# Modulation vectors of a hybrid DiT layer: weights as the stationary operand in plain float32

## The chip, the cores and the metric

The kernel runs on one core of a Trainium2 chip. The metric is the device time of one execution in microseconds (us), median of the runs shown. Engines are named as in the profile: PE (matmuls), PEld (PE's weight loads, which overlap its matmuls), DVE (vector), ACT (scalar), POOL (GpSimd) and SP, which issues most of the DMAs.

## The reference

Two layers of a diffusion backbone act on 1024 latent tokens and 256 context tokens of width 1024. Each layer has one projection into three kinds of heads (latent attention, differential attention, a gated chunk MLP), an output projection, and a convolutional MLP. The change concerns the modulation: shift, scale and gate vectors (six of width 1024 for each layer) made from a condition vector for the latents and another one for the context.

```
s_c = jax.nn.silu(c)
s_cc = jax.nn.silu(c_ctx)
for l in range(DEPTH):
    mod = (s_c @ p["ada_w"] + p["ada_b"])[:, None, :]
    modc = (s_cc @ p["ada_w"] + p["ada_b"])[None, None, :]
    x, xc = layer(x, xc, mod, modc, rows, cols, p, l, l < DEPTH - 1)

def layer(x, xc, mod, modc, ...):
    sh1, sc1, g1, sh2, sc2, g2 = jnp.split(mod, 6, axis=-1)
    y, yc = mixer(x * (1.0 + sc1) + sh1, xc * (1.0 + csc1) + csh1, ...)
    x = layer_norm(DN_ALPHA * x + g1 * y, ...)
    x = layer_norm(DN_ALPHA * x + g2 * conv_ffn(x * (1.0 + sc2) + sh2, p), ...)
```

`ada_w` is 1024 x 6144 for each layer, 50 MB in float32 for both, and it is multiplied by two vectors only.

## The kernel before, in words

**Numbers.** Nearly all matrix products are written as three matmuls of type float32r. Each operand is split into a high part (a rounding copy, mostly on ACT, line 460 `copy`) and a low part (the full value minus the high one, on DVE or POOL, line 457 `low`). Line 447 (`mm`) issues every matmul of this kind. Transposes and a few small products run in plain float32: `ident`, `sel64` (64 moving columns), `sumj`, and the mixing product of the chunk MLP (`wsT`, 64 moving columns).

**Order.** The program is a list of tasks. Each names the engines it may run on with an estimated time, the buffers that it reads and writes, and a key. A scheduler (`Sched.run`) plays the list through with these estimates when the program is built. It gives each task to an engine and thereby fixes the order of instructions on each engine. A changed estimate or a removed task moves other tasks too, among them those that can run on either DVE or POOL.

**Modulation.** The 48 pieces (two layers, six vectors, four quarters) are made by `mod_piece`. A piece is 1024 x 256 of `ada_w`. Its weights are loaded, split into high and low, and are the moving operand: 16 matmuls of 256 columns, in which the stationary operand is `s4`, the silu of both condition vectors as high and low (four columns, shown as `region,s` in the profile). The result, four rows by 256, is copied from PSUM by ACT (`m4`), and two matmuls with the 4 x 2 matrix `sel4` (4 rows, moving 2 columns, plain float32) bring it to columns and add high and low. DVE adds the bias (line 715).

The pieces stand at two kinds of places. Eight of layer 0 (scale and shift of the first norm) are made at the start, in `first_hT`, in blocks of 128 x 1024 (`raws` given), between the first tokens and the first projection weights, whose products need them. The other 40 are filled into the two attention stages (24 into layer 0's, 16 into layer 1's) in blocks of 128 x 512, of which each is loaded, split and multiplied by a task of its own. There PE also has score matmuls, transposes of the probabilities (line 1252) and the products with the values; DVE takes the running minimum of the scores out of PSUM (line 1183) and makes low parts; ACT does the exponentials (line 1188) and high parts.

The instructions of an engine run in the order of the program, so whatever stands behind a waiting matmul on PE waits too.

Of the kernel before, what the change touches and what calls it, by code (L numbers as in the profile page):

```python
# [10 lines left out]
F32 = mybir.dt.float32  # L11
F32R = mybir.dt.float32r
# [8 lines left out]
P = 128  # L21
# [312 lines left out]
def dve_t(n, per=1.042e-3, extra=0.0):  # L334
    return {"dve": per * n + 0.07 + extra}
# [32 lines left out]
def mm_t(count, n):  # L368
    return {"pe": count * max(0.11, 0.4167e-3 * n + 0.0027)}
# [21 lines left out]
class Kern:  # L391
# [248 lines left out]
    def setup(self):  # L640
        nc, c, i = self.nc, self.cst, self.i

        def load(name, shape, key=0):
            t = c.tile(shape, F32, tag=name, name=name)
            self.dma(lambda: t, lambda: i[name], 4 * P * int(np.prod(shape[1:])), w=[name], key=key)
            return t

        cc = load("cT", [P, KD, 2])
        s = c.tile([P, KD, 2], F32, tag="silu", name="silu")
        self.s4 = c.tile([P, KD, 4], F32R, tag="s4", name="s4")  # L650
        self.task(act_t(16), lambda e: nc.scalar.activation(s, cc, AF.Silu), ["cT"], ["silu"])
        self.task(dve_t(16), lambda e: nc.vector.tensor_copy(self.s4[:, :, 0:2], s), ["silu"], ["s4a"])
        self.task(dve_t(16), lambda e: self.low(nc.vector, self.s4[:, :, 2:4], s, self.s4[:, :, 0:2]), ["silu", "s4a"], ["s4"])
        self.sel4 = load("sel4", [4, 2])
        self.modv, self.lnv, self.adab, self.inw = [], [], [], {}
        for l in range(DEPTH):
            self.modv.append(c.tile([P, 6, KD, 2], F32, tag=f"modv{l}", name="modv"))
            t = c.tile([P, 6, KD], F32, tag=f"adab{l}", name="adab")
            self.dma(lambda t=t: t, lambda l=l: i["ada_b"][l], 4 * P * 48, w=[("adab", l)], key=300 * l)
            self.adab.append(t)  # L660
            t = c.tile([P, 4, KD], F32, tag=f"lnv{l}", name="lnv")
            self.dma(lambda t=t: t, lambda l=l: i["lnv"][l], 4 * P * 32, w=[("lnv", l)], key=300)
            self.lnv.append(t)
        self.cv = c.tile([P, 2 * NF, 4], F32, tag="conv", name="conv")
        for name, shape in (("ident", [P, P]), ("sumj", [P, P]), ("sel64", [P, 64])):
            setattr(self, name, load(name, shape, 200))
        self.identr = c.tile([P, P], F32R, tag="identr", name="identr")
        self.task(dve_t(P), lambda e: nc.vector.tensor_copy(self.identr, self.ident), ["ident"], ["identr"], key=200)
        d = self.dr
        self.zd = d.tile([NTOK, 768], F32, tag="zd", name="zd")  # L670
        self.yt = d.tile([NTOK, 512], F32, tag="yt", name="yt")
        self.oT = d.tile([512, NTOK], F32, tag="oT", name="oT")
        self.n1 = d.tile([NTOK, D], F32, tag="n1", name="n1")
        self.n2 = d.tile([SEQ, D], F32, tag="n2", name="n2")
        self.da = [d.tile([7, P, NP, HALF], F32, tag=f"da{l}", name="da") for l in range(DEPTH)]
        self.dc = d.tile([7, P, NP, P], F32, tag="dc", name="dc")
        self.db = [d.tile([4, NP, P, HALF], F32, tag=f"db{l}", name="db") for l in range(DEPTH)]
# [3 lines left out]
        return self.i["ada_w"][l, QUADS[n // 4], n % 4, h]  # L681

    def mod_piece(self, l, n, key=0, raws=None):
        nc = self.nc
        self.s.what = f"mod{l}"
        j, q = QUADS[n // 4], n % 4
        if raws:
            w = [self.weight(None, 1024, self.L, k=4, raw=raws[h]) for h in range(2)]
        else:
            src = [self.mod_src(l, n, h)[:, a:a + 512] for h in range(2) for a in (0, 512)]  # L690
            w = [self.weight(x, 512, self.M, k=2, key=key, acq=True) for x in src]
        kk = KD // len(w)
        ps, m4, pm = self.bank(), self.H(), self.bank(F32, (P, 2, 2))
        for h in range(len(w)):
            def go(e, h=h):
                for k in range(kk):
                    hi, lo = w[h][0][k]()
                    a = self.s4[:, kk * h + k]
                    self.mm(ps[:4, :256], a, hi, h + k == 0, False)
                    self.mm(ps[:4, :256], a, lo, False, kk * h + k == KD - 1)  # L700

            self.task(mm_t(2 * kk, 256), go, ["s4"] + w[h][1], [ps], key=key, acq=[m4] if h == 0 else ())
        self.task(act_t(256), lambda e: self.copy(m4[:4], ps[:4, :256]), [ps], [m4], key=key)

        def sel(e):
            for k in range(2):
                self.mm(pm[:, k], m4[:4, k * P:(k + 1) * P], self.sel4)

        self.task({"pe": 0.25}, sel, [m4, "sel4"], [pm], key=key)
        ks = slice(2 * q, 2 * q + 2)  # L710
        o = self.modv[l][:, j, ks]
        tok = ("modv", l, j, q)

        def fin(e):
            nc.vector.tensor_tensor(out=o, in0=pm.t, in1=self.adab[l][:, j, ks].unsqueeze(2).to_broadcast([P, 2, 2]), op=ALU.add)
            if j in (1, 4):
                nc.vector.tensor_scalar(o, o, 1.0, None, op0=ALU.add)

        self.task({"dve": 0.15}, fin, [pm, ("adab", l)], [tok], key=key)
# [1236 lines left out]
def _arrays(x, c, ctx, c_ctx, ada_w, ada_b, w_in, mla_gq, mla_wuq, mla_gkv, mla_wukv,  # L1956
            diff_lq1, diff_lk1, diff_lq2, diff_lk2, diff_subln_g, sgu_ln_g, sgu_ln_b, sgu_ws, sgu_bs,
            w_o, ln1_g, ln1_b, ffn_wup, ffn_convw, ffn_convb, ffn_wdown, ln2_g, ln2_b):
    L = DEPTH
    a = {}  # L1960
    a["x"], a["ctx"] = x[0], ctx[0]
    a["cT"] = _cols(np.stack([c[0], c_ctx])).transpose(0, 2, 1)
    a["xT"] = np.concatenate([ctx[0], x[0]]).reshape(NTOK, KD, P).transpose(2, 1, 0)
    a["ada_w"] = ada_w.reshape(L, 2, 4, P, 6, 4, 256).transpose(0, 4, 5, 1, 3, 2, 6).reshape(L, 6, 4, 2, P, 1024)
    a["ada_b"] = _cols(ada_b.reshape(L, 6, D)).transpose(1, 0, 2, 3)
    for name in ZCH:
        b, n = ZOFF[name], ZN[name]
        a["w_in_" + name] = w_in[:, :, b:b + n].reshape(L, KD, P, n).transpose(0, 2, 1, 3).reshape(L, P, KD * n)
    wq = mla_wuq.reshape(L, 3, P, NH, 192)
    r = wq[..., 128:]  # L1970
    sw = r.reshape(L, 3, P, NH, 2, 2, 16)[..., ::-1, :].reshape(r.shape)
    a["wq"] = np.concatenate([wq[..., :128], r, sw], -1).transpose(0, 3, 2, 1, 4).reshape(L, NH, P, 768)
    wkv = mla_wukv.reshape(L, 2, P, NH, 256)
    a["wk"] = wkv[..., :128].transpose(0, 3, 2, 1, 4).reshape(L, NH, P, 256)
    a["wv"] = wkv[..., 128:].reshape(L, 2, P, 2, 2, 128).transpose(0, 3, 2, 1, 4, 5).reshape(L, 2, P, 512)
    a["gq"] = _cols(mla_gq).transpose(1, 0, 2)
    a["gkv"] = _cols(mla_gkv).transpose(1, 0, 2)
    a["dl"] = np.stack([diff_lq1, diff_lq2, diff_lk1, diff_lk2], 1)
    a["subln"] = diff_subln_g
    a["sgu_gb"] = np.concatenate([sgu_ln_g, sgu_ln_b], 1)  # L1980
    a["wsT"] = sgu_ws.transpose(0, 3, 1, 2)
    a["bs"] = sgu_bs.transpose(0, 2, 1)
    wo = np.zeros((L, 35, P, 256), np.float32)
    wo[:, :32] = w_o.reshape(L, KD, P, 4, 256).transpose(0, 1, 3, 2, 4).reshape(L, 32, P, 256)
    a["w_o"] = wo.reshape(L, 7, 5, P, 256).transpose(0, 1, 3, 2, 4).reshape(L, 7, P, 1280)
    ln = np.stack([ln1_g, ln1_b, ln2_g, ln2_b], 1)
    a["lnr"] = ln
    a["lnv"] = _cols(ln).transpose(1, 0, 2, 3)
    a["wup"] = ffn_wup.reshape(L, 2, 4, P, 2, NF, P).transpose(0, 4, 1, 5, 3, 2, 6).reshape(L, 2, 2, NF, P, 512)
    cw = np.concatenate([ffn_convw, ffn_convb[:, None]], 1)  # L1990
    a["conv"] = cw.reshape(L, 4, 2, NF, P).transpose(0, 4, 3, 2, 1).reshape(L, P, 2 * NF, 4)
    a["w_down"] = ffn_wdown.reshape(L, NP, 2, P, 2, HALF).transpose(0, 2, 4, 1, 3, 5)
    a["dtab"], a["ktab"], a["cst"] = _rope_tables()
    eye = np.eye(P, dtype=np.float32)
    a["ident"] = eye
    a["sumj"] = np.tile(np.eye(64, dtype=np.float32), (2, 2))
    a["sel64"] = np.tile(np.eye(64, dtype=np.float32), (2, 1))
    a["sel4"] = np.tile(np.eye(2, dtype=np.float32), (2, 1))
    return {k: np.ascontiguousarray(v) for k, v in a.items()}


# [12 lines left out]
```

## Time and profile before

| | |
|---|---|
| median of 3 runs | 3407.99 us (3407.11 to 3412.31) |
| the profiled execution: its time | 3411.25 us |
| its span, first to last instruction | 3409.5 us |
| PE busy | 3186.5 us, 93% of the span |
| DVE, ACT, POOL busy | 79%, 49%, 30% |
| granted TensorE clock, mean | 0.967 of full speed |

The profiled execution is 3.3 us above the median, and 1.75 us of it lie outside its span. The granted clock has two levels here, 1.00 (2.4 GHz) and 0.50 (1.2 GHz); values between are means over a stretch.

### The profile page before, as it was taken

To read this page: it belongs to the slowest core of one execution; us is meant where nothing else is said; L and a number is where in the kernel's file an instruction comes from. 1 tells how busy PE (TensorE), PEld (TensorE's weight loads), DVE (VectorE), ACT (ScalarE), POOL (GpSimd) and SP (SyncE) were. 2 spreads that over 40 slices of the span, in tenths; PEclk is the share of its full clock that TensorE was granted. 3 is DMA by queue.
4 is the path that set the end of the run, shared out by engine and by line. 5 is a ranking of instruction groups with operands and counts; after the bars stand their busy time and mean duration, and the time that the engine had idled before them with its cause. 6 is when DMAs were issued, how large, how long until landed. Compare 5 with 4: busy or idle time off the path is not lost. (4 is left out here: it accounts for less than half of the span.)

```text
span 3409.5 us, 53373 instructions
## 1 busy us (share of the span) xinstructions
PE 3186.5 (93%) x18953; PEld 2785.7 (82%) x18953; DVE 2700.5 (79%) x6407; ACT 1677.3 (49%) x2944; POOL 1028.0 (30%) x631
## 2 busy tenths in 40 slices
PE   7999898998988999999999999989999889999997
PEld 5998887887987888887877898878889867877775
DVE  7567887999768787886687757988998788888687
ACT  5125665666244444544444325665662455545542
POOL 3002554543112111121133302554532232322143
PEclk9999998999999999999999999999999999999998
DMA  6214443442312223225663314353423122323672
GB/s 242 72 52 112 118 124 99 126 108 86 121 69 70 89 72 101 87 86 180 210 204 130 116 58 123 92 135 87 119 88 127 62 80 96 107 98 105 229 258 99
DMA packets 258548, 395.40 MB, mean 116 GB/s; under 512 B 63976, under 2 KB 115688, under 8 KB 258280
## 3 DMA queue, kind: packets, MB, share of 16 engines
q1 hardware_dynamic: 240872, 345.84, 31.4%
q0 software_dynamic: 17408, 46.14, 5.9%
q8 instruction: 149, 2.44, 0.3%
q14 instruction: 119, 0.97, 0.1%
HBM read 311.61 MB, written 126.42 MB: 128 GB/s over the span
## 5 line engine op out<-in xcount | busy, mean ns | idle before, releaser
L447 PE MATMUL t<-region 128*128 128x512 f32 (+4 forms) x15631 | 2853.0, 341 | 137.8 <-DVE region L457 55.0
L447 PEld LDWEIGHTS t<-region 128*128 128x128 f32 x15631 | 2442.1, 192 | 480.0 <-DVE region L457 69.2
L457 DVE TENSOR_TENSOR region<-region 128x512 fp32r<-128x512 f32 (+6 forms) x873 | 760.0, 893 | 176.2 <-ACT region L460 122.7
L460 ACT ACTIVATE region<-region 128x512 fp32r<-128x512 f32 (+4 forms) x944 | 593.9, 663 | 382.8 <-PE t L447 132.5
L460 ACT ACTIVATE region<-t 128x512 fp32r<-128x512 f32 (+4 forms) x948 | 462.1, 514 | 600.0 <-PE t L447 386.3
L457 POOL TENSOR_TENSOR region<-region 128x512 fp32r<-128x512 f32 (+7 forms) x283 | 392.3, 1398 | 1109.3 <-ACT region L460 714.8
L1480 POOL TENSOR_TENSOR region<-region 128x512 f32<-128x512 f32 (+3 forms) x132 | 248.6, 1889 | 823.6 <-DVE region L1667 518.5
L1188 ACT ACTIVATE region<-region,q 128x1280 f32<-128x1280 f32 (+1 forms) x216 | 273.5, 1267 | 175.7 <-DVE q L1187 169.7
L1183 DVE TENSOR_SCALAR_CACHE_REDUCE region<-t 128x512 f32<-128x512 f32 (+1 forms) x600 | 333.7, 584 | 21.3 <-PE t L447 19.1
L457 DVE TENSOR_TENSOR region<-t,region 128x512 fp32r<-128x512 f32 (+1 forms) x529 | 296.9, 595 | 52.8 <-ACT region L460 50.9
L1667 DVE SCALAR_TENSOR_TENSOR region<-region,conv 128x1023 f32<-128x1023 f32 x176 | 231.6, 1325 | 36.7 <-ACT region L1665 36.5
L1480 DVE TENSOR_TENSOR region<-region 128x512 f32<-128x512 f32 (+3 forms) x301 | 226.3, 770 | 2.5 <-DMA da<-region 1.4
L1252 PE MATMUL t<-ident,region 128*128 128x128 f32 x1312 | 184.8, 285 | 24.2 <-DVE region L1225 8.1
L1228 POOL TENSOR_TENSOR region<-region 128x1280 f32<-128x1280 f32 (+1 forms) x68 | 186.8, 2746 | 5.7
L1665 ACT ACTIVATE region<-region,conv 128x1024 f32<-128x1024 f32 x88 | 109.2, 1241 | 159.5 <-DVE region L1648 148.3
L1252 PEld LDWEIGHTS t<-ident,region 128*128 128x128 f32 x1312 | 154.9, 147 | 31.8 <-DVE region L1183 11.0
L1227 POOL TENSOR_SCALAR region<-region,q 128x1280 f32<-128x1280 f32 (+1 forms) x68 | 84.5, 1242 | 210.6 <-DVE q L1222 137.7
L447 PE MATMUL t<-region,s 128*4 128x256 f32 x768 | 119.1, 291 | 17.0 <-DVE region L457 9.2
L447 PEld LDWEIGHTS t<-region,s 128*4 128x4 f32 x768 | 64.6, 87 | 47.4 <-DVE region L457 12.5
L548 POOL TENSOR_TENSOR region<-region 128x1024 f32<-128x1024 f32 x26 | 73.7, 2847 | 95.9 <-DMA region<-n 67.7
L1008 DVE TENSOR_TENSOR region<-t,region 128x256 f32<-128x256 f32 x32 | 13.6, 424 | 107.4 <-PE t L447 107.4
L548 DVE TENSOR_TENSOR region<-region 128x1024 f32<-128x1024 f32 x34 | 62.3, 1841 | 18.2 <-DMA region<-n 17.7
(134 smaller groups left out, 1803.5 us busy)
## 6 DMA issues: line engine op xcount, KB each, us to landing
region<-in_wup SPq DMA_DIRECT2D x176, 256.0 KB, 3.0
region<-in_ada_w SPq DMA_DIRECT2D x160, 256.0 KB, 3.1
da<-region SPq DMA_DIRECT2D x154, 256.0 KB, 3.0
region<-da SPq DMA_DIRECT2D x154, 256.0 KB, 4.1
db<-in_w_down POOLq DMA_DIRECT2D x24, 1408.0 KB, 7.5
region<-db SPq DMA_DIRECT2D x88, 256.0 KB, 4.1
region<-in_w_down SPq DMA_DIRECT2D x66, 256.0 KB, 3.9
n<-region SPq DMA_DIRECT2D x26, 512.0 KB, 3.0
```

Source lines behind the costliest of these rows:

```text
L447: self.nc.tensor.matmul(ps, a, b, start=start, stop=stop, skip_group_check=again)
L457: eng.tensor_tensor(out=out, in0=full, in1=hi.bitcast(F32), op=ALU.subtract)
L460: self.nc.scalar.activation(out, in_, AF.Copy, **kw)
L548: self.task(engs or pool_t(D), lambda e, row=row, op=op: self.vec[e].tensor_tensor(out=x[:, :D], in0=x[:, :D], in1=row.t, op=op), [x, row] ...
L1183: self.task(dve_t(b - a), lambda e: nc.vector.tensor_scalar(p[:, a:b], ps[:, :b - a], -scale, None, op0=ALU.mult, op1=ALU.min, accum_out=n ...
L1188: self.task(act_t(nk, 0.19), lambda e: nc.scalar.activation(p[:, :nk], p[:, :nk], AF.Exp, bias=m.t, scale=-1.0, accum_out=s.t), [p, m], [p ...
L1227: nc.gpsimd.tensor_scalar(p2[:, :nk], p2[:, :nk], cc.t, 0.0, op0=ALU.mult, op1=ALU.add)
L1228: nc.gpsimd.tensor_tensor(out=p1[:, :nk], in0=p1[:, :nk], in1=p2[:, :nk], op=ALU.add)
L1252: nc.tensor.transpose(ps[:, u, j * P:(j + 1) * P], B[key][j][:, (kt + u) * P:(kt + u + 1) * P], self.ident)
L1480: self.task(engs or either(n), lambda e: self.vec[e].tensor_tensor(out=o(), in0=a(), in1=b(), op=op), r, w, **kw)
L1665: self.task(act_t(n, 0.15), lambda e: nc.scalar.activation(t.t, u(0, n), AF.Identity, scale=c[:, 1:2], bias=c[:, 3:4]), r + ["conv"], [t])
L1667: self.task(dve_t(n - 1, extra=0.06), lambda e, d=d: nc.vector.scalar_tensor_tensor(t[:, 1 - d:n - d], u(d, n - 1 + d), c[:, 2 * d:2 * d + ...
```

## The change

The split of the modulation weights, the four-row product, its copy and the selecting product are taken out. Each 128 x 128 block of `ada_w` is now itself the stationary operand, in plain float32, and the moving operand is the silu of both condition vectors: two columns. A piece is 16 matmuls (two groups of 128 outputs, eight blocks along the contraction each) that add up in PSUM, in one task that waits for all of the piece's blocks. DVE's bias add stays. `s4`, its high and low part, and `sel4` go. The estimate of PE's time for a piece, on which the scheduler works, becomes 1.8 us (it was 16 times 0.11 and 0.25).

```
-        self.s4 = c.tile([P, KD, 4], F32R, tag="s4", name="s4")
+        self.silu = s
-        self.task(dve_t(16), lambda e: nc.vector.tensor_copy(self.s4[:, :, 0:2], s), ["silu"], ["s4a"])
-        self.task(dve_t(16), lambda e: self.low(nc.vector, self.s4[:, :, 2:4], s, self.s4[:, :, 0:2]), ["silu", "s4a"], ["s4"])
-        self.sel4 = load("sel4", [4, 2])
...
-        if raws:
-            w = [self.weight(None, 1024, self.L, k=4, raw=raws[h]) for h in range(2)]
-        else:
-            src = [self.mod_src(l, n, h)[:, a:a + 512] for h in range(2) for a in (0, 512)]
-            w = [self.weight(x, 512, self.M, k=2, key=key, acq=True) for x in src]
-        kk = KD // len(w)
-        ps, m4, pm = self.bank(), self.H(), self.bank(F32, (P, 2, 2))
-        for h in range(len(w)):
-            def go(e, h=h):
-                for k in range(kk):
-                    hi, lo = w[h][0][k]()
-                    a = self.s4[:, kk * h + k]
-                    self.mm(ps[:4, :256], a, hi, h + k == 0, False)
-                    self.mm(ps[:4, :256], a, lo, False, kk * h + k == KD - 1)
-
-            self.task(mm_t(2 * kk, 256), go, ["s4"] + w[h][1], [ps], key=key, acq=[m4] if h == 0 else ())
-        self.task(act_t(256), lambda e: self.copy(m4[:4], ps[:4, :256]), [ps], [m4], key=key)
-
-        def sel(e):
-            for k in range(2):
-                self.mm(pm[:, k], m4[:4, k * P:(k + 1) * P], self.sel4)
-
-        self.task({"pe": 0.25}, sel, [m4, "sel4"], [pm], key=key)
+        if not raws:
+            raws = [self.load(self.mod_src(l, n, h)[:, a:a + 512], 512, self.M, key) for h in range(2) for a in (0, 512)]
+        kk = KD // len(raws)
+        pm = self.bank(F32, (P, 2, 2))
+
+        def go(e):
+            for c in range(2):
+                for k in range(KD):
+                    o = k % kk * 256 + c * P
+                    self.mm(pm[:, c], raws[k // kk][:, o:o + P], self.silu[:, k], k == 0, k == KD - 1)
+
+        self.task({"pe": 1.8}, go, ["silu", *raws], [pm], key=key)
```

The order on PE at the start of the program, before (`s_70` is the four-column operand, `sel_71` the selecting matrix; the rows of 512 columns are the first projection):

```order
L447 MATMUL t<-region,s_70 4x256 x24
L447 MATMUL t<-sel_71,region 128x2 x2
L447 MATMUL t<-region,s_70 4x256 x16
L447 MATMUL t<-sel_71,region 128x2 x2
L447 MATMUL t<-region,s_70 4x256 x16
L447 MATMUL t<-sel_71,region 128x2 x2
L447 MATMUL t<-region,s_70 4x256 x8
L447 MATMUL t<-sel_71,region 128x2 x2
L447 MATMUL t<-region 128x512 x36
L447 MATMUL t<-region,s_70 4x256 x24
L447 MATMUL t<-sel_71,region 128x2 x2
```

The same place on PE after the change:

```order
L447 MATMUL t<-silu,region 128x2 x64
L447 MATMUL t<-region 128x512 x36
L447 MATMUL t<-silu,region 128x2 x48
L447 MATMUL t<-region 128x512 x36
L447 MATMUL t<-silu,region 128x2 x16
L447 MATMUL t<-region 128x512 x96
```

The eight pieces stand in three groups now, of four, three and one, with nothing between the pieces of a group.

On PE at the entry of layer 0's attention, where the first fillers stand, before:

```order
L1168 MATMUL t<-identr,region 128x128 x12
L447 MATMUL t<-region,s_70 4x256 x20
L447 MATMUL t<-sel_71,region 128x2 x2
L985 MATMUL t<-ident,region 128x128 x6
L447 MATMUL t<-region,s_70 4x256 x16
L447 MATMUL t<-sel_71,region 128x2 x2
L447 MATMUL t<-region 128x512 x12
L447 MATMUL t<-region 128x256 x24
```

And after (the line numbers behind the edit are lower by 13):

```order
L1155 MATMUL t<-identr,region 128x128 x12
L447 MATMUL t<-silu,region 128x2 x48
L972 MATMUL t<-ident,region 128x128 x6
L447 MATMUL t<-region 128x512 x12
L447 MATMUL t<-region 128x256 x24
L447 MATMUL t<-region,sumj 128x256
```

Three pieces come in one run here. The other 37 pieces of the attention stages stand alone as runs of 16; before, most came as runs of 4 to 8 with other matmuls between. On DVE the program began with the two halves of `s4` and the low parts of the first pieces:

```order
L652 CAST s_70<-silu 128x8x2
L457 TENSOR_TENSOR s_70<-silu,s_70 128x8x2
L457 TENSOR_TENSOR region<-region 128x1024 x4
L715 TENSOR_TENSOR modv<-t,adab 128x4
L717 TENSOR_SCALAR modv<-modv 128x4
L457 TENSOR_TENSOR region<-region 128x1024 x2
```

Now it begins with the bias adds:

```order
L702 TENSOR_TENSOR modv<-t,adab 128x4
L704 TENSOR_SCALAR modv<-modv 128x4
L702 TENSOR_TENSOR modv<-t,adab 128x4 x2
L704 TENSOR_SCALAR modv<-modv 128x4
L702 TENSOR_TENSOR modv<-t,adab 128x4
L825 CAST region<-region 128x768
```

Over the whole program the order has these counts before and after: low parts of 128 x 512 on DVE 625 and 562, on POOL 160 and 63; of 128 x 1024 on DVE 19 and 5; high parts on ACT of 128 x 512 785 and 625, of 128 x 1024 24 and 8; copies of four rows on ACT 48 and none; matmuls with `s4` 768 and none, with `sel4` 96 and none, with the silu as moving operand none and 768. The rest is the same, but for some tasks that changed between DVE and POOL.

## Rows read from the trace of the kernel before

**Rows 1.** The page, part 1: engine, busy us (share of the span), instructions.

```profile
PE 3186.5 (93%) x18953; PEld 2785.7 (82%) x18953; DVE 2700.5 (79%) x6407; ACT 1677.3 (49%) x2944; POOL 1028.0 (30%) x631
```

**Rows 2.** Busy us by stretch: start, both attention stages; then clock, DMA share, GB/s.

```profile
0.00:60.00 60.00, 48.45 (x258) 35.20 (x259) 40.08 (x56) 35.62 (x46) 10.99 (x9) 0.94 0.86 309
255.00:830.00 575.00, 527.73 (x3691) 472.51 (x3689) 486.56 (x1481) 358.20 (x720) 257.08 (x174) 0.95 0.41 111
2055.00:2560.00 505.00, 470.54 (x3280) 420.69 (x3279) 451.60 (x1314) 312.57 (x593) 225.06 (x141) 0.97 0.41 109
```

**Rows 3.** Groups by form, whole span: count | busy us, mean ns | idle before.

```profile
L457 DVE TENSOR_TENSOR region<-region 128x512 fp32r<-128x512 f32 x625 | 564.3, 923 | 149.0 <-ACT region L460 113.2 <-DMA region<-db 12.7 <-PE t L447 12.2
L460 ACT ACTIVATE region<-region 128x512 fp32r<-128x512 f32 x785 | 470.0, 626 | 305.9 <-DVE region L1480 131.0 <-PE t L447 100.1 <-DMA region<-in_w_down 16.4
L457 POOL TENSOR_TENSOR region<-region 128x512 fp32r<-128x512 f32 x160 | 227.9, 1434 | 523.7 <-ACT region L460 446.1 <-PE t L447 51.9 <-DVE q L484 10.9
...
L447 PE MATMUL t<-region,s 128*4 128x256 f32 x768 | 119.1, 291 | 17.0 <-DVE region L457 9.2 <-ACT region L460 7.7
...
L447 PE MATMUL t<-sel,region 4*128 4x2 f32 x192 | 29.7, 255 | 4.1 <-ACT region L460 3.4 <-DVE region L457 0.5
...
L460 ACT ACTIVATE region<-t 4x256 f32<-4x256 f32 x48 | 17.5, 366 | 29.9 <-PE t L447 29.7
```

**Rows 4.** Tile s (`s4`): idle ahead of its instructions by releaser, us and times.

```profile
  DVE region L457: 21.7, 28
  ACT region L460: 15.5, 4
```

**Rows 5.** Timeline of PEld at 48 to 58 us: start, us taken, what, count.

```profile
49.70 1.94 PEld L447 LDWEIGHTS t<-region,s 128*4 128x4 f32 x16
51.88 0.52 PEld L447 LDWEIGHTS t<-sel,region 4*128 4x128 f32 x4 [0.24 <-issue]
```

**Rows 6.** Tile of the selecting matrices: ns of one, least/median/most; first and last start.

```profile
L447 PEld LDWEIGHTS t<-sel,region x336: 181/187/338, 12.8 to 2560.4; 4*128 4x128 f32 x96, 128*128 128x128 f32 x72
```

**Rows 7.** Groups of PE by form from 85 to 91 us.

```profile
L447 PE MATMUL t<-region 128*128 128x64 f32 x24 | 5.6, 423 | 7.5 <-issue 7.5
```

**Rows 8.** One-us windows around it, columns as in rows 2.

```profile
86.00:87.00 1.00, 1.00 (x7) 1.00 (x6) 1.00 (x9) 0.00 (x0) 0.00 (x0) 0.50 0.00 0
...
90.00:91.00 1.00, 1.00 (x5) 1.00 (x5) 1.00 (x6) 0.00 (x0) 0.00 (x0) 0.50 0.00 0
...
94.00:95.00 1.00, 1.00 (x4) 0.71 (x4) 1.00 (x5) 0.00 (x0) 1.00 (x1) 0.50 0.73 169
95.00:96.00 1.00, 1.00 (x6) 0.82 (x5) 1.00 (x3) 0.00 (x0) 0.82 (x1) 0.93 0.98 379
```

**Rows 9.** Groups of PE by form from 91.2 to 95 us.

```profile
L447 PE MATMUL t<-region 128*128 128x512 f32 x11 | 4.9, 628 | 0.0
```

**Rows 10.** The same from 64 to 77 us.

```profile
L447 PE MATMUL t<-region 128*128 128x512 f32 x57 | 13.2, 391 | 1.4 <-DVE region L457 1.4
```

**Rows 11.** Timeline of PEld at 463 to 472 us.

```profile
465.56 0.42 PEld L447 LDWEIGHTS t<-region 128*128 128x128 f32 x3 [1.65 <-DVE region L457]
466.12 0.52 PEld L447 LDWEIGHTS t<-sel,region 4*128 4x128 f32 x4
...
466.89 0.91 PEld L447 LDWEIGHTS t<-sel,region 128*128 128x128 f32 x4
```

**Rows 12.** One-us windows there, columns as in rows 2.

```profile
466.00:467.00 1.00, 1.00 (x8) 0.87 (x7) 1.00 (x6) 0.67 (x3) 0.00 (x0) 1.00 0.00 0
467.00:468.00 1.00, 1.00 (x8) 0.96 (x7) 1.00 (x7) 0.58 (x1) 0.00 (x0) 0.60 0.04 9
```

**Rows 13.** Five-us windows behind a long wait of PE in layer 0's attention.

```profile
565.00:570.00 5.00, 0.00 (x0) 0.00 (x0) 0.00 (x0) 0.00 (x0) 3.10 (x3) 0.62 0.34 118
570.00:575.00 5.00, 4.58 (x25) 4.59 (x26) 0.15 (x1) 2.16 (x5) 2.83 (x3) 0.50 0.64 228
575.00:580.00 5.00, 5.00 (x39) 5.00 (x38) 2.23 (x6) 1.93 (x6) 0.37 (x1) 0.86 0.00 0
```

More of the change, by code (lines that the diff above doesn't have):

```diff
@@ L1997, in _arrays @@
     a["sel64"] = np.tile(np.eye(64, dtype=np.float32), (2, 1))
-    a["sel4"] = np.tile(np.eye(2, dtype=np.float32), (2, 1))
     return {k: np.ascontiguousarray(v) for k, v in a.items()}
```

## The prediction

> **What bounds the kernel now.** I first read the page's busy line [rows 1]: PE is busy for 93% of the span, DVE for 79%, and the two can't be told apart as bounds by that alone. The stretches in which the pieces lie say more [rows 2]. In layer 0's attention PE is busy 527.7 of 575 us and in layer 1's 470.5 of 505, so it idles for 47 and 34 us there, 82 together. DVE is busy 486.6 and 451.6. PE is the nearest to its limit, but it waits often, mostly for low and high parts. At the start PE has 48.5 of 60 us. So what a piece costs on PE is paid almost in full, unless it falls into one of those waits, and what it costs on DVE, ACT and POOL counts only where PE waits for them.
>
> **What goes on DVE, ACT and POOL.** From the counts of the order and the means of [rows 3]: 160 high parts of 0.626 us and 48 copies of 0.366 leave ACT (118 us, and 16 larger ones at the start), 63 low parts of 0.923 leave DVE (58 us, and 14 larger ones), 97 of 1.434 leave POOL (139 us). None of this is on PE. What is on PE's path is the wait for those parts: ahead of matmuls with `s4` an engine sat idle for 21.7 us on DVE's low parts and 15.5 us, in four cases, on ACT's high parts [rows 4]. I count the 21.7; I take the 15.5 as the wait for the first weights, which remains, since a block must land in either version.
>
> **What a piece costs on PE, at full clock.** Before: 16 loads of the four-column operand take 1.94 us, and the selecting product, two matmuls that the trace shows as four records, 0.53 from its first load to the next instruction [rows 5] (its count, 192 records for 96 matmuls, is in [rows 3]). Together 2.47 us. After: 16 plain float32 matmuls with 128 x 128 weights and two moving columns. The nearest row is the selecting product itself: plain float32, 128 weight columns, two moving columns. Its four records take 0.52 us, and the last load lasts 0.19 [rows 6], so three starts take 0.33, or 0.11 us for a record. Two records to a matmul make 32 for a piece: 3.5 us, 3.6 with the end of the last. That is 1.15 us more than before, and 48 pieces make **+55 us**. The bounds are 0.11 and 0.13 (0.52 by four): +55 and +81. I take the lower one, since a long run has one end only.
>
> **What the clock does.** The granted clock is the term I am least sure of and the largest. At 85 us PE, after a wait, works through 24 records of the chunk MLP's mixing product, plain float32 with 64 moving columns [rows 7]. PE and PEld are busy all through 86 to 91 us and the clock stays at 0.50. Then 512-column matmuls follow, and the clock is back at about 95 us [rows 8]. So an engine that is busy loading weights, with few moving columns, was not given the full clock, while dense moving columns were. A fall from the full level without an idle PE is near that at 467 us: three matmuls behind a wait of 1.65 us, the selecting product, two matmuls, the first of a 64-column product [rows 11], and the clock falls while PE is busy 1.00 in both windows [rows 12]. The new piece has two moving columns for a matmul, for 3.6 us on end, where the old one streamed 256 columns each time. I expect the clock to fall in or right behind nine pieces in ten.
>
> In the Trainium skill, the page "TensorE: Matmul & The Clock Gate", section "Why this matters for your kernels", asks for a TensorE that is kept busy without gaps, and the clock then stays up. By that rule a run of back-to-back matmuls would cost nothing here, and the sum would be that of the first rival. The rows at 86 to 91 us don't agree with the rule as a busy share alone.
>
> The price of a fall: 512-column matmuls take 4.9/11 = 0.45 us at the lower level [rows 9] and 13.2/57 = 0.23 at the upper one [rows 10]. The lower level lasted over some 4 us of such work at 91 to 95 us, and over 6 us at 570 to 576 (4.6 busy in one window; a mean of 0.86 in the next is 1.4 us) [rows 13]. Half of that is lost: 2 to 3 us, I take 2.5. In attention, 40 pieces x 0.9 x 2.5 = 90 us. At the start the eight pieces stand in runs of four, three and one: three falls, 7.5 us, and what lies behind the fall within the runs goes at about half pace too. Seven pieces at half pace throughout would be 7 x 32 x 0.11 = 25 us; I take 11, since a run begins at the full level. Together **+108 us**. The bounds are 0, if the clock holds, and about 190, if half of each piece in attention is also at half pace (40 x 1.75 = 70 more, and the start's other 14).
>
> **What is absorbed.** A later PE finds its operands ready. Of the 82 us that PE idles in attention I let two thirds go, 55 us: the 21.7 of [rows 4] and 33 more of waits on parts, exponentials and minima, since DVE, ACT and POOL have less to do in these stages and PE more. At the start PE idles 11.6 of 60 us, part of which is the first weights' landing, and 7.5 us at 85 us, where it waits for DVE's chain [rows 7]; I let 12 go. Together **-67 us**. The bounds are 22 (the direct waits alone) and 101 (all of it).
>
> A piece's task now waits for all four blocks, and behind it on PE stand score matmuls and value products, for which DVE and ACT wait. I cost this at nothing, because the blocks only have to land: the DMA share in these stages is 0.41 [rows 2]. Without that cover it would be one landing, some us, for a piece. The two instructions for `s4` and one small DMA at the start lie ahead of the first weights' landing and are worth nothing.
>
> **The sum.** 55 + 108 - 67 = +96 us on the profiled execution's 3411.25, so 3507. That execution is 3.3 us above the median, so against the median I say **3504 us**, 2.8% slower.
>
> **Rivals.** *The clock holds.* For it: PE is busy without a gap in a piece, and no row of before has a long run with two columns at the full level. Against it: 86 to 91 us. Then the sum is 55 less what is absorbed, with the direct waits alone 22, so +33, and around +20 with some more: 3415 to 3441 us.
>
> *The clock holds and the other engines were the bound (faster).* The place is the attention stages. If PE's waits there are the work of DVE, ACT and POOL, which lose 58, 118 and 139 us, they go with it. PE's work alone then sets the end: 528 + 24 x 1.15 = 555 of 575 us, 470.5 + 16 x 1.15 = 489 of 505, with 7 us at the start -43 us at the most, and half of that, 3388 us, as the likely price. It decides for faster once more than 55 us of waits are freed and the clock stays up. Against it: only 22 of PE's waits are ahead of the pieces' own matmuls.
>
> *The clock falls early and the pieces themselves run at half pace.* A piece then adds up to 3.5 us beyond the 3.6. With half of that, 48 x 1.75 = 84 us, and 10 more of absorbed waits, it is +170: 3578 us. For it: three pieces stand in one run at the entry of attention and seven of eight in two runs at the start. Against it: single pieces begin at the full level, with dense matmuls ahead.
>
> *No change to be seen.* What is absorbed equals what is added, with the clock holding: 3401 to 3415.
>
> **How the numbers follow.** A change of under 0.2%, 7 us, can't be told from none here. Chances: forecast 0.58 (its own range 3450 to 3555), half pace within the pieces 0.13, clock holds 0.13, no change 0.07, faster 0.09. So slower 0.84, same 0.07, faster 0.09. The range from 3410 to 3580 us leaves out the faster case, most of no change and the upper end of the half-pace case, under 2 in 10.
>
> **What would show it.** In the profile after: 1536 PE records on the silu, with loads 0.11 us apart at the full level; if they come in 0.06, or as one record for a matmul, the +55 is wrong. The mean clock below 0.967, at about 0.93 to 0.95, with stretches at 0.50 right behind pieces in attention; if the windows behind a piece stay at 1.00, the +108 is wrong and the first rival holds. PE's busy time up by some 160 us, and its idle time in attention down from 82 to about 30; if idle stays at 82, too much was absorbed. DVE busy down by 58 to 80 us and ACT by about 130, with no gain from it. The MLP stages unchanged; if they move, something else is at work.

## The result, and the profile after

The changed kernel takes 3533.7 us (median of 4 runs, 3529.8 to 3542.4) against 3409.8 us before (4 runs): 1.0367 times as long, 95% interval 1.0344 to 1.0389, slower by 124 us. The profiled execution took 3529.8 us with a span of 3528.0, so 118.5 us more than the span of before.

The page's busy line of the changed kernel, as in [rows 1]:

```profile
PE 3326.7 (94%) x19529; PEld 2958.8 (84%) x19529; DVE 2620.8 (74%) x6311; ACT 1564.4 (44%) x2727; POOL 898.6 (25%) x543
```

The three engines that were to be relieved are: DVE by 79.7 us, ACT by 112.9, POOL by 129.4. PE is busy 140.2 us longer, and the span is up by 118.5: PE's idle time over the whole span fell only from 223.0 to 201.3 us.

Groups of the changed kernel by form (count | busy us, mean ns | idle before), whole span:

```profile
L447 PE MATMUL t<-region 128*128 128x512 f32 x7079 | 1761.8, 404 | 104.6 <-ACT region L460 39.7 <-DVE region L457 33.5 <-DVE region L1170 12.2
L447 PE MATMUL t<-region 128*128 128x256 f32 x7496 | 1030.7, 293 | 42.2 <-DVE region L457 28.6 <-ACT region L460 7.8 <-DVE region L1170 2.7
L447 PE MATMUL t<-silu,region 128*128 128x2 f32 x1536 | 210.3, 272 | 5.8 <-DMA region<-in_ada_w 5.4 <-ACT region L460 0.4
```

The pieces took PE 119.1 + 29.7 = 148.8 us before [rows 3] and take 210.3 now, 61.5 more. The other 78.7 us of PE's 140.2 are in matmuls whose number did not change: the same work, done more slowly.

The mean granted clock fell from 0.967 to 0.947. The clock record has 69 stretches at 0.50, 374 us in all; before it was 37 and 224 us. Within layer 0's attention, one piece on PEld (timeline: start, us taken, what, count):

```profile
705.35 2.21 PEld L1239 LDWEIGHTS t<-ident,region 128*128 128x128 f32 x20
707.52 3.65 PEld L447 LDWEIGHTS t<-silu,region 128*128 128x128 f32 x32
711.10 3.38 PEld L447 LDWEIGHTS t<-region 128*128 128x128 f32 x20
714.42 1.53 PEld L1239 LDWEIGHTS t<-ident,region 128*128 128x128 f32 x8
...
717.85 2.34 PEld L447 LDWEIGHTS t<-region 128*128 128x128 f32 x19
```

And the one-us windows there, columns as in [rows 2]:

```profile
710.00:711.00 1.00, 1.00 (x11) 1.00 (x11) 1.00 (x2) 0.00 (x0) 0.00 (x0) 1.00 0.60 172
711.00:712.00 1.00, 1.00 (x10) 1.00 (x10) 0.97 (x5) 0.00 (x0) 0.00 (x0) 1.00 0.91 369
712.00:713.00 1.00, 1.00 (x8) 1.00 (x7) 0.82 (x4) 0.00 (x0) 0.00 (x0) 0.67 1.08 389
713.00:714.00 1.00, 1.00 (x7) 1.00 (x6) 0.00 (x0) 0.00 (x0) 0.00 (x0) 0.50 1.12 242
714.00:715.00 1.00, 1.00 (x7) 1.00 (x7) 0.00 (x0) 0.19 (x1) 0.00 (x0) 0.50 0.85 193
715.00:716.00 1.00, 1.00 (x7) 1.00 (x7) 0.33 (x1) 0.93 (x2) 0.00 (x0) 0.62 1.12 248
```

PE is busy 1.00 in every one of these windows, without a gap, before the piece, in it and behind it. The piece takes 3.65 us, and the clock falls about 1 us behind its end, while dense work runs. The price is to be seen in the loads of that dense work: 20 of them take 3.38 us right behind the piece, and 19 take 2.34 us at 717.85 us, with the clock back. This piece is typical. From the entry of layer 0's attention on, the 40 pieces make 38 unbroken runs of loads on PEld, and in 31 of the 38 a stretch at 0.50 begins within the run (11 times) or within 2 us behind its end (20 times). The start of the program shows the other form (timeline of PEld):

```profile
5.37 27.38 PEld L447 LDWEIGHTS t<-silu,region 128*128 128x128 f32 x128 [5.37 <-issue]
33.63 0.29 PEld L447 LDWEIGHTS t<-region 128*128 128x128 f32 x1 [0.88 <-issue]
37.16 10.69 PEld L447 LDWEIGHTS t<-region 128*128 128x128 f32 x35 [3.24 <-DVE region L457]
47.89 15.63 PEld L447 LDWEIGHTS t<-silu,region 128*128 128x128 f32 x96
```

The first four pieces go at 27.38/128 = 0.21 us a record from end to end, the pace of the lower level, and the first projection matmul comes at 33.7 us instead of 23.0 (timeline of PE in the kernel before):

```profile
23.01 0.50 PE L447 MATMUL t<-region 128*128 128x512 f32 x1 [1.26 <-ACT region L460]
```

The three pieces that stand in one run at the entry of layer 0's attention show the lower pace as well, for most of their length: 0.19 us a record.

```profile
303.35 18.02 PEld L447 LDWEIGHTS t<-silu,region 128*128 128x128 f32 x96
```

Both attention stages, in windows that end with the stage in this execution (they begin 30 and 81 us later than before):

```profile
330.00:904.00 574.00, 544.43 (x3722) 508.30 (x3721) 447.55 (x1354) 295.56 (x573) 187.29 (x116) 0.90 0.37 100
2171.00:2675.00 504.00, 478.65 (x3273) 443.36 (x3272) 403.48 (x1204) 266.38 (x487) 173.37 (x98) 0.92 0.36 99
```

PE idles 29.6 and 25.3 us in them. The same two stages of the kernel before lie at 300 to 847 and 2090 to 2567 us, where it idled 48.8 and 35.0 us:

```profile
300.00:847.00 547.00, 498.21 (x3489) 445.03 (x3488) 470.76 (x1399) 342.85 (x677) 259.71 (x171) 0.95 0.39 106
2090.00:2567.00 477.00, 442.05 (x3092) 393.51 (x3092) 432.10 (x1231) 299.01 (x556) 220.85 (x136) 0.97 0.40 106
```

Each stage is 27 us longer. Where the 118.5 us arise, from the starts of the same matmuls in the traces (first of 320 columns, first and last matmuls of each attention stage, end), beside the experiment `wide128` that follows:

| stretch | after less before, us | wide128 less before, us |
|---|---|---|
| start to the first projections of 320 columns | +18.9 | 0.0 |
| to the first attention stage | +11.5 | +2.3 |
| layer 0's attention | +27.2 | -4.1 |
| output projection, MLP of layer 0, input of layer 1 | +23.2 | +22.9 |
| layer 1's attention | +27.9 | +4.3 |
| the rest | +9.8 | +13.4 |
| sum | +118.5 | +38.8 |

### The profile page after: what moved, and what is told of

Its sections match the earlier page's. It is cut to its first block, busy times and chain, and to the rows that moved or that the text cites. A ratio compares the mean times of both kernels' runs of the same rounds, so it can differ in the third digit from the quotient of the medians.

```text
span 3528.0 us, 53886 instructions
## 1 busy us (share of the span) xinstructions
PE 3326.7 (94%) x19529; PEld 2958.8 (84%) x19529; DVE 2620.8 (74%) x6311; ACT 1564.4 (44%) x2727; POOL 898.6 (25%) x543
## 4 chain that ended last, share of the span: by engine, by line
PE 57%; DVE 13%; ACT 2%; issue 2%; POOL 1%; DMA 1%; SPq 0%; DVEq 0%; ACTq 0%; POOLq 0%
PE t L447 54%; DVE region L457 4%; DVE region L1467 2%; PE t L1239 1%; ACT region L460 1%; DVE region L1170 1%; DVE region L466 1%; DVE region L1654 1%; POOL region L457 1%; DVE region L548 0%; DVE t L1621 0%; DVE region L1768 0%; ACT region L1652 0%; DMA region<-in_lnr 0%; DVE region L1749 0%
## 5 line engine op out<-in xcount | busy, mean ns | idle before, releaser
L447 PE MATMUL t<-region 128*128 128x256 f32 (+4 forms) x15631 | 2894.5, 345 | 156.1 <-DVE region L457 62.1
L447 PEld LDWEIGHTS t<-region 128*128 128x128 f32 x15631 | 2482.0, 196 | 507.9 <-DVE region L457 73.0
L457 DVE TENSOR_TENSOR region<-region 128x512 fp32r<-128x512 f32 (+6 forms) x800 | 686.2, 882 | 163.0 <-ACT region L460 125.7
L460 ACT ACTIVATE region<-t 128x512 fp32r<-128x512 f32 (+3 forms) x907 | 448.7, 523 | 730.1 <-PE t L447 451.1
L460 ACT ACTIVATE region<-region 128x512 fp32r<-128x512 f32 (+4 forms) x768 | 480.1, 662 | 398.6 <-PE t L447 145.0
L457 POOL TENSOR_TENSOR region<-region 128x512 fp32r<-128x512 f32 (+6 forms) x180 | 253.0, 1415 | 994.8 <-ACT region L460 481.8
L1467 POOL TENSOR_TENSOR region<-region 128x512 f32<-128x512 f32 (+2 forms) x134 | 247.0, 1848 | 857.0 <-DVE region L1654 453.2
L1467 DVE TENSOR_TENSOR region<-region 128x512 f32<-128x512 f32 (+2 forms) x299 | 231.9, 793 | 2.3 <-DMA region<-in_wup 1.1
L447 PEld LDWEIGHTS t<-silu,region 128*128 128x128 f32 x1536 | 210.6, 224 | 7.2 <-issue 5.4
L447 PE MATMUL t<-silu,region 128*128 128x2 f32 x1536 | 210.3, 272 | 5.8 <-DMA region<-in_ada_w 5.4
L1214 POOL TENSOR_SCALAR region<-region,q 128x1280 f32<-128x1280 f32 (+1 forms) x69 | 85.5, 1239 | 487.7 <-DVE q L1209 290.0
```

What stands on the lines that cost most here:

```text
L447: self.nc.tensor.matmul(ps, a, b, start=start, stop=stop, skip_group_check=again)
L457: eng.tensor_tensor(out=out, in0=full, in1=hi.bitcast(F32), op=ALU.subtract)
L460: self.nc.scalar.activation(out, in_, AF.Copy, **kw)
L1214: nc.gpsimd.tensor_scalar(p2[:, :nk], p2[:, :nk], cc.t, 0.0, op0=ALU.mult, op1=ALU.add)
L1467: self.task(engs or either(n), lambda e: self.vec[e].tensor_tensor(out=o(), in0=a(), in1=b(), op=op), r, w, **kw)
```

## Experiments

**The clock alone.** The decisive experiment keeps every instruction of the change in its place on its engine and makes the moving operand wider: the two columns of the silu, read 64 times over.

```
-        pm = self.bank(F32, (P, 2, 2))
+        pm = self.bank(F32, (P, 2, 64, 2))
...
-        self.mm(pm[:, c], raws[k // kk][:, o:o + P], self.silu[:, k], k == 0, k == KD - 1)
+        self.mm(pm[:, c], raws[k // kk][:, o:o + P], self.silu[:, k].unsqueeze(1).to_broadcast([P, 64, 2]), k == 0, k == KD - 1)
```

> The changed kernel with the silu of both condition vectors repeated 64 times in the moving operand: 128 moving columns instead of 2, the same weight loads, the same order on every engine; 126 of the 128 result columns are not used. Theory (the clock): of the 118.5 us more in the span, 61 are PE's time in the pieces (210.3 us for 119.1 and 29.7) and 79 are other matmuls at the lower clock, less 22 of idle time. With 128 columns the loads still come 0.11 us apart, but the clock should hold: PE busy down by 70 to 100 us, mean clock back to 0.965 or more, time 3430 to 3460 us. Rival (the pieces' PE time and the new order are the whole cost): no fewer falls or no gain from fewer, 3520 to 3550 us.

Measured: 3451.5 us, 1.0118 times before (1.0103 to 1.0133), 82 us less than the change. The busy line of its page:

```profile
PE 3233.0 (94%) x19529; PEld 2867.1 (83%) x19529; DVE 2619.2 (76%) x6311; ACT 1561.2 (45%) x2727; POOL 899.5 (26%) x543
```

And its span with the mean granted clock, from the list of cores:

```profile
core 0: 3448.2 us, clock 0.971
```

The order of instructions on each of the five rows of its profile (PE, PEld, DVE, ACT, POOL) is that of the change, one for one. With 64 times the columns, PE is busy 93.7 us less. The start and the three pieces at the entry of attention in its timeline of PEld:

```profile
5.37 15.79 PEld L447 LDWEIGHTS t<-silu,region 128*128 128x128 f32 x128 [5.37 <-issue]
22.15 0.19 PEld L447 LDWEIGHTS t<-region 128*128 128x128 f32 x1 [0.98 <-issue]
...
35.03 10.91 PEld L447 LDWEIGHTS t<-silu,region 128*128 128x128 f32 x96
...
284.48 10.79 PEld L447 LDWEIGHTS t<-silu,region 128*128 128x128 f32 x96
```

And the pieces' loads within layer 0's attention, grouped by tile (least, median and most ns of one; first and last start), in the change and then with 128 columns:

```profile
L447 PEld LDWEIGHTS t<-silu,region x672: 186/192/338, 348.4 to 851.6; 128*128 128x128 f32 x168
L447 PEld LDWEIGHTS t<-silu,region x672: 186/191/192, 320.4 to 793.1; 128*128 128x128 f32 x168
```

Both attention stages in its windows:

```profile
302.00:845.00 543.00, 508.30 (x3725) 472.59 (x3723) 447.09 (x1356) 294.30 (x574) 188.04 (x117) 0.97 0.39 106
2111.00:2592.00 481.00, 452.18 (x3278) 419.44 (x3278) 402.97 (x1199) 266.15 (x487) 173.40 (x98) 0.98 0.39 104
```

A piece in attention now has no load at the lower pace (192 ns at the most; the change has up to 338 there). The 128 loads at the start take 15.79 us instead of 27.38, and 96 take 10.91, 0.114 each, as priced; at the entry of attention 96 take 10.79 instead of 18.02. There are 33 stretches at 0.50, 199 us, and none begins in or within 2 us behind any of the 38 runs of pieces. By the table above, the start, the entry and both attention stages give back all that they had lost but 2.5 us, and the stages without pieces keep their loss. So the clock theory holds, and its rival fell: 82 of the 124 us are the clock's.

**The weights as moving operand, without split.** Here a two-column stationary operand in plain float32 meets 256 moving columns.

```
-                    hi, lo = w[h][0][k]()
-                    a = self.s4[:, kk * h + k]
-                    self.mm(ps[:4, :256], a, hi, h + k == 0, False)
-                    self.mm(ps[:4, :256], a, lo, False, kk * h + k == KD - 1)
+                    self.mm(ps[:2, :256], self.silu[:, kk * h + k], raws[h][:, k * 256:(k + 1) * 256], h + k == 0, kk * h + k == KD - 1)
```

> The weights stay the moving operand as in the kernel before (256 columns), but in plain float32, without split; the stationary operand is the two-column silu, one task for each block, and the two-row result is brought to columns by the selecting product with a 2 x 2 identity. PE has 8 matmuls of two records of 0.215 us and the selecting product, 4.0 us for a piece. Theory (the clock): no more falls than before, so 3425 to 3470 us although a piece takes longer on PE than in the change (3.6 at full clock, 4.4 measured). Rival (PE's time in the pieces): as slow as the change or slower, 3530 to 3560 us.

Measured: 3473.1 us, 1.0182 (1.0167 to 1.0197), a little over the expected range. Its clock is 0.974 with 31 stretches at 0.50, and it is 61 us faster than the change although its pieces take PE 191.3 + 29.3 = 220.6 us, 10 more than there. The rows of the pieces by form, here and in `wide128`:

```profile
L447 PE MATMUL t<-region,silu 128*2 128x256 f32 x768 | 191.3, 386 | 10.2 <-DMA region<-in_ada_w 8.7 <-DVE q L1179 0.7 <-DVE region L1175 0.6
L447 PE MATMUL t<-sel,region 2*128 2x2 f32 x192 | 29.3, 253 | 0.8 <-ACT region L460 0.5 <-DVE region L457 0.3
```

```profile
L447 PE MATMUL t<-silu,region 128*128 128x128 f32 x1536 | 180.6, 276 | 5.7 <-DMA region<-in_ada_w 5.4 <-ACT region L460 0.2
```

Its order differs from the change's. Of the 59 us between the two spans, 27 lie ahead of layer 0's attention and 21 in the two attention stages, where the pieces are; 11 lie between these stages, where none stands, and are the order's. So here a longer PE time at the full clock was cheaper than a shorter one that lowers it, though order can have a part in the 21. Against `wide128` its pieces cost PE 40 us more and the time is 22 us longer, in another order again.

**Half of the change each.** `mod_piece` takes the new form with `raws` (the start) or without (attention), the other half as before.

> The new form in the two attention stages alone (40 pieces); the eight pieces at the start are as before. If the start's delay (the first matmul of 320 columns comes 18.9 us later, the first of the attention stage 30.4 us) is carried to the end, 3500 to 3520 us. Rival: that delay is made up for later, then 3525 to 3540 us.

> The new form in the eight pieces at the start alone; the 40 of the attention stages are as before. If the start's delay is carried to the end, 3422 to 3445 us, slower than before; the first 64 matmuls should take 27 us again, 0.21 us a record. Rival: it is made up for in the waits behind it, 3405 to 3415 us.

Measured: 3499.8 us for attention alone (1.0255, 1.0238 to 1.0272; clock 0.943), 0.2 us below its range, and 3436.0 for the start alone (1.0076, 1.0061 to 1.0091). At the start alone the first projection of 320 columns comes 19.8 us later than before, and the end 23.1 us later; the first 64 matmuls take 27.4 us again. That is the number of the theory, but the delay does not simply run through: the last matmuls of layer 0's attention come 11.9 us later than before and the first of layer 1's 11.0, so some 8 us are made up for, and 9 us arise again behind layer 1's attention, where no piece stands. In one order, the change less `wide128`, the start's delay was not made up for by the first attention stage: 18.9 us at the first projections of 320 columns, 28 there, of which the three pieces at the entry add 7. The two halves sum to 113 us of the 124, each in an order of its own.

**A piece in four parts.** Two columns as in the change, but four tasks of four matmuls, so that others can come between.

```
+        for c in range(2):
+            for g in range(2):
+                def go(e, c=c, g=g):
+                    for k in range(4 * g, 4 * g + 4):
+                        o = k % kk * 256 + c * P
+                        self.mm(pm[:, c], raws[k // kk][:, o:o + P], self.silu[:, k], k == 0, k == KD - 1)
+
+                self.task({"pe": 0.9}, go, ["silu", *raws], [pm], key=key)
```

> The changed kernel, two moving columns, with each piece cut into four tasks of four matmuls (0.9 us at full clock), so that other matmuls come between them in the attention stages; at the start they still stand in runs. Theory (the clock falls because a piece is one unbroken run of few moving columns): fewer falls in attention, a mean clock of 0.955 to 0.965 and 3460 to 3500 us. Rival (every two-column matmul holds the clock down, however it is spread, or the clock is not the cost): 3520 to 3550 us.

> The same four tasks for a piece with 128 moving columns. By the clock theory cutting has nothing left to save, so 3435 to 3465 us, as the uncut one with 128 columns (3451.5). If it is faster than 3430 us, the length of the run on PE (others waiting behind it) had a cost of its own beside the clock.

Measured: 3488.2 us with two columns (1.0229, 1.0214 to 1.0245; clock 0.955, 51 stretches), and 3426.9 with 128 (1.0047, 1.0032 to 1.0062). These two have the same order on every engine, one for one, so they are a second comparison of the columns alone: 61 us. The order itself is worth 25 us against the uncut version, by the pair with 128 columns (3451.5 less 3426.9), so of the 45 us by which `spread` is faster than the change some 20 are left for the clock.

In the attention stages, runs of the pieces' matmuls on PEld with nothing between, and how many of them have the begin of a stretch at 0.50 within them or within 2 us behind:

| matmuls in the run | `spread`: runs, with a fall | the change: runs, with a fall |
|---|---|---|
| 4 | 81, 6 | |
| 8 or 12 | 20, 8 | |
| 16 | 5, 5 | 37, 30 |
| more | 2, 1 | 1, 1 |

So cutting made falls rarer and did not end them; with 128 columns none begins at a piece, cut or uncut. The start, where the first four pieces stay one run, again comes 20 us late. The second version is faster than its range, and by its own expectation would speak for a cost of the run's length beside the clock. Since its order differs from that of `wide128`, and the next runs show orders to differ by as much, that reading is not shown.

**Order alone.** The kernel before with another estimate for a task of the pieces, and the version with 128 columns with other estimates: the work is the same, the order isn't.

```
-        self.task({"pe": 0.25}, sel, [m4, "sel4"], [pm], key=key)
+        self.task({"pe": 0.55}, sel, [m4, "sel4"], [pm], key=key)
```

> The kernel before, with no work changed; only the estimate of the selecting product on which the scheduler works is 0.55 us instead of 0.25, which changes the order on all engines, in the MLP stages too. Theory (the 30 us that the wide version still loses in the MLP stages come from another order there): 3415 to 3445 us. Rival (order is worth little; the loss there is due to something that the change did): 3405 to 3415 us.

> The kernel before with the estimate of the selecting product at 0.40 us, a third order of its work (0.25: 3411, 0.55: 3434 us). If the order of before lies at the lower end by selection, 3415 to 3445 us; if 3434 was an outlier, 3400 to 3415 us.

> 128 moving columns and the scheduler's estimate for a piece at 3.6 us, what it takes on PE, instead of 1.8; the order changes everywhere. If the wrong estimate costs something, 3415 to 3440 us; if orders differ by chance only, 3425 to 3475 us, either side of 3451.5.

> 128 moving columns, estimate of a piece 2.2 us: another order of the same work. The versions with 128 columns gave 3427 to 3452 us so far. Theory (PE's 50 us more in the pieces is absorbed in the attention stages, and the order decides the rest): between 3395 and 3455 us. Rival (a fixed cost of the new form remains): 3425 us or more in all three of these.

> As the one before with 2.4 us: theory 3395 to 3455 us, rival 3425 us or more.

> As the one before with 2.8 us: theory 3395 to 3455 us, rival 3425 us or more.

| kernel | time, us | against before, with interval |
|---|---|---|
| before, estimate 0.25 us (as it was) | 3411 | |
| before, 0.40 us (`reest40`) | 3412.7 | 1.0009 (0.9999 to 1.0018) |
| before, 0.55 us (`reest`) | 3434.1 | 1.0065 (1.0050 to 1.0080) |
| 128 columns, 1.8 us (`wide128`) | 3451.5 | 1.0118 (1.0103 to 1.0133) |
| 128 columns, 2.2 us | 3410.1 | 1.0001 (0.9991 to 1.0010) |
| 128 columns, 2.4 us | 3431.8 | 1.0062 (1.0046 to 1.0079) |
| 128 columns, 2.8 us | 3406.5 | 0.9984 (0.9975 to 0.9994) |
| 128 columns, 3.6 us | 3429.4 | 1.0047 (1.0030 to 1.0064) |

An order by itself is worth up to 23 us in the kernel before and 45 us in the version with 128 columns, so differences of that size between the times of versions with different orders say nothing of the work. The rival of a fixed cost of the new form fell with 3410.1 and 3406.5 us. The last is the fastest of all; it is faster than before by 0.16%, clear of its interval but less than what one would call a gain of the form. By its expectation `reest40`, at 3412.7 us, makes the 3434.1 of `reest` the outlier. The 3429.4 of `wide_t36` lies in the range of its theory and in that of its rival; the right estimate for a piece is not the best one, since 2.2 and 2.8 us gave less.

## Why the prediction was right

The forecast was 3504 us, and 3533.7 came, inside the range from 3410 to 3580 and inside the forecast's own. The mechanism, a clock that falls at the pieces, was right. Three of the sum's terms were off, and their errors cancelled in part: PE's busy time was to rise by 163 us and rose by 140.2, its idle time was to fall by 67 and fell by 21.7. That the total is only 22 us off (118.5 in the span for 96) is luck to that extent.

*What a piece costs on PE* was put at +55 us, 3.6 for 2.47 us a piece, and is +61.5: 4.38 (210.3/48) for 3.10 (148.8/48). Both prices were too low, by 0.8 and 0.6 us, and the difference came near because of that. The price of a record, 0.11 us at the full level, held (3.65 us for 32 in the timeline at 707.52). The excess after the change is records at the lower level: over all pieces the loads take 211 us, where 0.114 us a record would make 175. Why a piece of before took 3.10 us stays open.

*What the clock does* was put at +108 us, with 19 of it at the start. PE's other matmuls took 78.7 us longer; with the first run's own records at half pace, some 13 us (27.4 less 14.2), that is about 92. By the direct comparison, the clock is worth 82 us of time (3533.7 less 3451.5). The price of a fall was about right: 41 stretches at 0.50 begin in the two attention windows of the change, 194 us in all or 4.7 each, and half of that is 2.4 us. A fall at nine pieces in ten was near the 31 of 38 runs too. What the term left out are the falls of the kernel before: 15 stretches begin in its two windows, and only 10 in those of `wide128`. So there are 26 more than before, where the sum had 36. The Trainium skill, page "TensorE: Matmul & The Clock Gate", section "Why this matters for your kernels", asks for TensorE to be kept busy without long idle gaps between bursts; the windows from 710 to 716 us, busy 1.00 throughout and yet down to 0.50, show that this alone did not keep the clock here.

*What is absorbed* was put at -67 us and was the worst term. In attention PE's idle time fell from 83.8 to 54.9 us, by 29 instead of 55. Up to that point it fell by 9, and it rose by 14 between the attention stages and by 2 behind them, so over the whole span it fell by 21.7. The 21.7 us of direct waits in [rows 4], the same number by chance, add the idle time of two rows of the profile: 9.2 of them are PE's [rows 3], and the other 12.5 are PEld's, by this line of the page of before:

```profile
L447 PEld LDWEIGHTS t<-region,s 128*4 128x4 f32 x768 | 64.6, 87 | 47.4 <-DVE region L457 12.5
```

So for PE the lower bound of this term was 9 us, not 22.

*The MLP stages unchanged* was wrong. Between the two attention stages the kernel takes 24 us longer (windows of the changed kernel, then of the one before):

```profile
904.00:2171.00 1267.00, 1207.28 (x6811) 1057.27 (x6810) 920.34 (x1988) 535.95 (x899) 258.88 (x170) 0.98 0.35 113
```

```profile
847.00:2090.00 1243.00, 1197.45 (x6802) 1050.16 (x6801) 923.19 (x1987) 541.12 (x907) 257.02 (x169) 0.98 0.36 114
```

PE idles 59.7 us there instead of 45.6 and is busy 9.8 us longer. These stages hold no piece. `wide128`, which has the order of the change, loses the same 23 and 13 us there with the clock restored, while the same work with 128 columns, in the five orders of the table, takes from 1245 to 1280 us between the attention stages and from 835 to 856 behind them (before: 1244 and 843). So 33 us of the result go with the new order, which I had taken as neutral; the stretches that the sum speaks of have 85.5 us, for the 96 that it gives. Which of the moved instructions makes the MLP wait was not tried and stays open.

The rival *the clock holds* and the faster one need a clock at 1.00 behind the pieces, and the windows at 712 to 716 us show it at 0.50. With 128 columns, where it does hold, attention as a whole takes 0.2 us more than before (-4.1 and +4.3), and in the four other orders from 1 us more to 16 less. So the faster rival's floor of -36 us there was out of reach, although DVE, ACT and POOL had all their relief. The rival of half pace within the pieces came true for the long runs: all of the first 128 records (0.21 us each) and much of the two runs of 96 (0.16 at 47.89 us, 0.19 at 303.35). Of the 37 single pieces ten have the fall within them and lose 0.6 to 2.7 us each. Together that is 36 us of loads, where the rival had 84.

The rest of what was to be seen came: 1536 records, a mean clock of 0.947, DVE down by 80 us and ACT by 113 (130 was said) with no gain from it.

## What to carry to other kernels

Price a rearranged matmul by what it does to the clock of its neighbours, not only by its own duration: a run of matmuls that load many weights and move few columns can be busy without a gap and still leave the dense work behind it at half speed. Where the load sets the pace anyway, more moving columns were free up to the 128 that were tried, and repeating the few there are gave 82 us back here. And when a scheduler makes the order, measure the same work in another order or two before reading a per cent as the effect of a change.

## What the runs showed of the hardware

The granted clock reads 1.00 in the profile up to the first entry of its record, and the pace of the first instructions says otherwise: 0.21 us for a record from 5.4 to 32.8 us in the changed kernel, in a window that shows a clock of 1.00:

```profile
0.00:30.00 30.00, 24.60 (x116) 24.63 (x116) 0.82 (x5) 4.39 (x5) 0.20 (x4) 1.00 0.77 276
```

That first entry is a rise to 1.00, at 43.3 us; in `wide128` it comes at 8.4 us, and the loads go from 0.21 to 0.11 us there. At the start the pace of known instructions is the better witness.

At the full level 64 times the moving columns do not slow a run of plain float32 weight loads: 32 with 2 columns take 3.65 us at 707.52 us of the changed kernel, 96 with 128 columns take 10.91 us at 35.03 us of `wide128`, 0.114 us each in both.
